# A mixture-of-experts kernel: 8 KB runs for the output matrices, and another order inside a pair of experts

## The chip, the cores and the metric

The kernel runs on one core of one Trainium2 chip. A core has five engines: TensorE (PE in the profile; PEld are its weight loads), VectorE (DVE), ScalarE (ACT), GpSimd (POOL) and SyncE (SP), which here issues the DMAs. Sixteen DMA engines move data between HBM and the on-chip buffer. The metric is the device time of one execution in microseconds, from the first to the last instruction of the core, and of several runs the median.

## The reference

Two blocks follow each other on 256 tokens of 1024 floats: two hybrid layers (convolution, attention), then an attention layer with a mixture of experts. The change lies in the experts alone. Each token goes to 4 of 32 experts; each expert has an input matrix of 1024 x 2048 and an output matrix of 1024 x 1024, all float32 (12 MB an expert, 403 MB in all):

```python
def expert_block(args):
    xb, e = args
    hcat = xb @ w_in[e] + b_in[e]
    x_glu = jnp.minimum(hcat[:, :D_FF], SWIGLU_LIMIT)
    x_lin = jnp.clip(hcat[:, D_FF:], -SWIGLU_LIMIT, SWIGLU_LIMIT)
    act = x_glu * jax.nn.sigmoid(SWIGLU_ALPHA * x_glu) * (x_lin + 1)
    return act @ w_out[e] + b_out[e]

ys = lax.map(expert_block, (xs, block_exp)).reshape(n_rows, dm)
y = jax.ops.segment_sum(ys * row_gate[:, None].astype(ys.dtype), row_tok, num_segments=n + 1)[:n]
```

The rows of `xs` are the tokens sorted by expert; `row_gate` is the weight of the token at that expert. A residual and a final norm follow.

## The kernel before

All 256 tokens stay on the chip and the weights of all 32 experts are streamed through it once. `moe` (from L1252) goes through 16 pairs of experts; each expert has 64 places for tokens, and a pair's 128 places fill the 128 rows of a tile. A branch after pair 10 (`overflow`, L1433) handles an expert with more than 64 tokens; in the profiled execution its body isn't run.

A weight tile is 1 MB, 128 partitions x 2048 floats. A pair has 24 of them, in the order in which PE needs them: 8 input tiles of the first expert, 8 of the second, then 8 output tiles, the two experts taking turns. `mload` (L1221) issues one DMA for a tile on SP into the next of 19 buffers that go round (`mv`, `mhch`, `mhcl`, `mXM`, `mtb`, `mhh`, `mhl`, `mM`, `mkbT`, `mG`, two `mY`, a second `mv`, three `mr`, three `mw`); it has to wait until PE has read what that buffer held. An input tile is 128 rows of the matrix, so each partition gets one run of 8 KB. An output tile is 256 rows of 1024 floats: partition p gets row p and row 128 + p, two runs of 4 KB (L1242). The last pair (p == 15) has its output matrices cut by columns as well, in runs of 2 KB.

One pair (`pair`, L1362) does this:

- the input matmuls (L1377), 8 tiles of each expert. `hp` holds two PSUM tiles, the gate half (i = 0) and the linear half (i = 1); each has the left 512 columns in its partitions 0 to 63 and the right 512 in 64 to 127. The biases are put there before by matmuls with a one-hot column (`in_bias`, L1330);
- the swiglu of an expert on DVE and ACT: `g` (L1383), tanh (L1384), three steps of `ln` (L1385 to L1387);
- transposes of `ln` on PE (L1391) and a copy by ACT to `aT` (L1392); after the first expert also those of the gates, `gsT` (L1398);
- the dispatch of the next pair (`dispatch`, L1336; matmuls L1354): a one-hot matrix `sx`, made by DVE (L1346), picks the next pair's tokens into `xT`, copied by ACT (L1357);
- the output matmuls (L1427; L1417 in the last pair): `aT` of the first expert writes partitions 0 to 63 of `yp`, that of the second 64 to 127;
- the combine: DVE scales `yp` to `ys` (L1407), and matmuls with `gsT` add it to the four accumulators `y` of the tokens (L1291).

PE's matmuls are fp32, so that one matmul shows up as two instructions in the profile. Matmuls that write different halves of the partitions stand side by side in the array and run at the same time.

The order in the code is not the order on the engines. A scheduler reorders all instructions by the code's order, priorities and simulated times, and fixes a sequence for each engine; an engine then takes its instructions in that sequence and waits at one that isn't ready. Four PSUM buffers, used in turn, serve `hp`, the transposes, the dispatch and `yp`.

Of the kernel before, what the change touches and what calls it, by code (L numbers as in the profile page):

```python
# [8 lines left out]
F32 = mybir.dt.float32  # L9
# [20 lines left out]
class Net:  # L30
# [1191 lines left out]
    def mload(self):  # L1222
# [11 lines left out]
        else:  # L1234
# [7 lines left out]
            src = w.rearrange("(k p) n -> p k n", p=128)  # L1242
            dst = b.rearrange("p (k n) -> p k n", k=4 if p == 15 else 2)
# [117 lines left out]

    def pair(self, disp, nxt, oh, hp, tile_of, gt2, acc, steps=(), last=False):  # L1362
        nc, T = self.nc, self.tmp
        xT, gs = disp
        hs = [slice(0, 64), slice(64, 128)]
        aT = []
        for e in range(2):
            hg, hn = hp
            for k in range(8):
                if k == 4 and e == 0:  # L1370
                    for _ in steps:
                        pass
                w = tile_of()
                for i in range(2):
                    for h in range(2):
                        o = i * 1024 + h * 512
                        nc.tensor.matmul(hp[i][hs[h]], xT[:, k, hs[e]], w[:, o:o + 512], start=False, stop=(k == 7))  # L1377
            if e == 0:
                hp = self.in_bias(oh[1])
            g = T.tile([128, 512], F32, name="g", tag="g", bufs=TB)  # L1380
            th = self.modr[:, 1]
            ln = T.tile([128, 512], F32, name="ln", tag="ln", bufs=TB)
            nc.vector.tensor_scalar(g, hg, 7.0, None, op0=ALU.min)  # L1383
            nc.scalar.activation(th, g, AF.Tanh, scale=0.851)  # L1384
            nc.vector.tensor_scalar(ln, hn, 7.0, -7.0, op0=ALU.min, op1=ALU.max)  # L1385
            nc.vector.scalar_tensor_tensor(ln, ln, 1.0, g, op0=ALU.add, op1=ALU.mult)  # L1386
            nc.vector.scalar_tensor_tensor(ln, th, 1.0, ln, op0=ALU.add, op1=ALU.mult)  # L1387
            a = T.tile([128, 4, 128], F32, name="aT", tag="aT", bufs=2)
            p = self.mm_ps([128, 4, 128])
            for c in range(4):  # L1390
                nc.tensor.transpose(p[:, c], ln[:, c * 128:(c + 1) * 128], self.ident)  # L1391
            nc.scalar.activation(a, p, AF.Copy, scale=0.5)  # L1392
            aT.append(a)
            if e == 0:
                gsT = T.tile([128, 2, 128], F32, name="gsT", tag="gsT", bufs=1)
# [200 lines left out]
```

## Time and profile before

| what | value |
|---|---|
| median of 3 runs (lowest to highest) | 2032.47 us (2032.28 to 2037.36) |
| profiled execution: span | 2031.7 us |
| PE busy | 1901.2 us (94%) |
| DVE, ACT, POOL busy | 920.7, 613.0, 410.8 us |
| HBM read | 565.8 MB |
| expert stage | about 1070 us to the end |

The profiled execution's own time is its span; the median of the runs lies 0.8 us above. Matmul ends are modelled, so that a PE that is shown as busy may still wait a little inside. A wait that the profile gives to `issue` has no releaser that it shows. Shares of DMA can be a little over 1, since packets of one engine overlap.

### The profile page before, as it was taken

The page shows a single profiled execution, that of the slowest core. Times are in us where ns is not written, and L with a number is a line of the kernel's source. Part 1 is how long each engine was busy: PE and PEld are TensorE (multiplying, and loading weights), DVE is VectorE, ACT ScalarE, POOL GpSimd, SP SyncE. Part 2 cuts the span into 40 slices and gives each one's busy share as a digit, 9 for nine tenths or more (in the row PEclk, how much of TensorE's full clock was granted, in tenths as well). Part 3 has the DMA queues.
Part 4 walks back from the last instruction along what each step waited for, and adds up shares of the span by engine and source line. Part 5 has one row for each costly group of instructions (what it writes and reads, how often), then busy time and mean ns, then how long its engine had stood idle before and what let it go on. Part 6 is the DMA issues. An engine that isn't in the chain of part 4 may idle for free. (4 is left out here: it accounts for less than half of the span.)

```text
span 2031.7 us, 25905 instructions
## 1 busy us (share of the span) xinstructions
PE 1901.2 (94%) x10323; PEld 1187.0 (58%) x10323; DVE 920.7 (45%) x1728; ACT 613.0 (30%) x1099; POOL 410.8 (20%) x334
## 2 busy tenths in 40 slices
PE   6989999989899999799969999999999998999997
PEld 6878988978679889676644333333333333333332
DVE  6798787678876665778751111111111101110102
ACT  4646445546465454455541000000000000100001
POOL 3134346653245245312120000000000000000000
PEclk8989999999899999899989999999999998999999
DMA  6545544546456435455459999999999999999994
GB/s 222 185 137 167 179 153 157 198 169 210 160 169 221 140 128 198 148 171 151 160 202 371 394 405 415 418 419 416 416 416 416 417 418 416 416 416 416 417 416 150
DMA packets 153812, 568.59 MB, mean 280 GB/s; under 512 B 10603, under 2 KB 16747, under 8 KB 120918
## 3 DMA queue, kind: packets, MB, share of 16 engines
q1 hardware_dynamic: 145024, 540.69, 69.4%
q0 software_dynamic: 6912, 25.17, 3.7%
q8 instruction: 83, 1.36, 0.3%
q10 hardware_dynamic: 1750, 1.03, 0.2%
q14 instruction: 43, 0.35, 0.1%
HBM read 565.79 MB, written 1.05 MB: 279 GB/s over the span
## 5 line engine op out<-in xcount | busy, mean ns | idle before, releaser
L158 DVE TENSOR_TENSOR wl<-raw,wh 128x1024 fp32r<-128x1024 f32 (+3 forms) x255 | 343.4, 1350 | 126.7 <-ACT wh L156 122.5
L156 ACT ACTIVATE wh<-raw 128x1024 fp32r<-128x1024 f32 (+3 forms) x255 | 262.8, 1034 | 236.9 <-PE mm L181 221.3
L1384 ACT ACTIVATE modr<-g 128x512 f32<-128x512 f32 x32 | 20.1, 629 | 675.2 <-DVE g L1383 675.2
L1383 DVE TENSOR_SCALAR g<-mm 128x512 f32<-128x512 f32 x32 | 22.1, 692 | 441.3 <-PE mm L1377 441.3
L182 PE MATMUL mm<-hh,wl 128*128 128x256 f32 x768 | 220.7, 289 | 0.9 <-DVE wl L158 0.9
L181 PE MATMUL mm<-hl,wh 128*128 128x256 f32 x768 | 220.2, 287 | 0.0
L180 PE MATMUL mm<-hh,wh 128*128 128x256 f32 x768 | 219.8, 287 | 0.0
L1304 POOL PARTITION_BROADCAST mtb<-bi x1 | 1.3, 1306 | 919.8 <-PE mm L1377 919.8
L181 PE MATMUL mm<-wl,hh 128*128 128x512 f32 (+2 forms) x424 | 173.5, 410 | 12.9 <-DVE wl L158 12.8
L182 PE MATMUL mm<-wh,hl 128*128 128x512 f32 (+2 forms) x424 | 171.5, 405 | 2.1 <-DVE hl L216 1.2
L180 PE MATMUL mm<-wh,hh 128*128 128x512 f32 (+2 forms) x424 | 164.4, 410 | 5.8 <-ACT hh L248 2.7
L822 POOL TENSOR_TENSOR araw<-araw,tb 128x1024 f32<-128x1024 f32 x48 | 100.1, 2085 | 297.7 <-DVE part L818 126.2
L182 PEld LDWEIGHTS mm<-hh,wl 128*128 128x128 f32 x768 | 144.3, 189 | 7.5 <-issue 4.4
L180 PEld LDWEIGHTS mm<-hh,wh 128*128 128x128 f32 x768 | 144.9, 189 | 4.7 <-issue 4.2
L181 PEld LDWEIGHTS mm<-hl,wh 128*128 128x128 f32 x768 | 144.7, 188 | 3.4 <-issue 2.0
L1407 DVE TENSOR_TENSOR ys<-kaT,mm 128x512 f32<-128x512 f32 x16 | 11.0, 688 | 249.5 <-PE mm L1427 239.3
L181 PEld LDWEIGHTS mm<-wl,hh 128*128 128x128 f32 x424 | 85.9, 203 | 33.3 <-DVE wl L158 15.7
L180 PEld LDWEIGHTS mm<-wh,hh 128*128 128x128 f32 x424 | 85.3, 203 | 25.8 <-ACT hh L248 4.4
L182 PEld LDWEIGHTS mm<-wh,hl 128*128 128x128 f32 x424 | 85.7, 202 | 19.3 <-DVE hl L249 2.1
L1354 PE MATMUL mm<-modr,vb 128*128 128x128 f32 x512 | 73.9, 313 | 14.1 <-DVE lg L1189 13.5
L824 POOL TENSOR_TENSOR araw<-araw 128x512 f32<-128x512 f32 x48 | 85.6, 1783 | 3.8
L1354 PEld LDWEIGHTS mm<-modr,vb 128*128 128x128 f32 x512 | 72.2, 228 | 16.2 <-DVE lg L1189 13.7
(444 smaller groups left out, 3578.0 us busy)
## 6 DMA issues: line engine op xcount, KB each, us to landing
raw<-in_w_in_dram SPq DMA_DIRECT2D x84, 1024.0 KB, 5.1
mr<-in_w_in_dram SPq DMA_DIRECT2D x41, 1024.0 KB, 18.3
mw<-in_w_in_dram SPq DMA_DIRECT2D x39, 1024.0 KB, 20.0
mv<-in_w_in_dram SPq DMA_DIRECT2D x27, 1024.0 KB, 19.9
mY<-in_w_in_dram SPq DMA_DIRECT2D x26, 1024.0 KB, 19.8
araw<-in_w_ada_dram POOLq DMA_DIRECT2D x48, 512.0 KB, 4.3
mw<-in_w_out_dram SPq DMA_DIRECT2D x21, 1024.0 KB, 19.9
mr<-in_w_out_dram SPq DMA_DIRECT2D x19, 1024.0 KB, 19.3
```

What stands on the lines that cost most here:

```text
L156: nc.scalar.activation(wh, src, AF.Copy)
L158: eng.tensor_tensor(wl, src, wh.bitcast(F32), op=ALU.subtract)
L180: nc.tensor.matmul(out, sh, mh, start=first, stop=False, skip_group_check=skip)
L181: nc.tensor.matmul(out, sh, ml, start=False, stop=False, skip_group_check=skip)
L182: nc.tensor.matmul(out, sl, mh, start=False, stop=last, skip_group_check=skip)
L822: nc.gpsimd.tensor_tensor(raw, raw, cT[:, 0, kh * 4:kh * 4 + 4, None].to_broadcast([128, 4, 256]), op=ALU.mult)
L824: nc.gpsimd.tensor_tensor(raw[:, 0:2], raw[:, 0:2], raw[:, 2:4], op=ALU.add)
L1304: nc.gpsimd.partition_broadcast(gfin, self.bi[96:97], channels=128)
L1354: nc.tensor.matmul(p[:, j], self.h2[:, t, k * 128:(k + 1) * 128], sx[:, t].rearrange("p e c -> p (e c)"), start=(t == 0 and j == 0), stop= ...
L1383: nc.vector.tensor_scalar(g, hg, 7.0, None, op0=ALU.min)
L1384: nc.scalar.activation(th, g, AF.Tanh, scale=0.851)
L1407: nc.vector.tensor_tensor(ys[:, h], gt2[h], yp[h], op=ALU.mult)
```

## The change

Three things change, all in the expert stage.

First, an output tile (but for the last pair) is read as `(p k) n`: partition p gets rows 2p and 2p + 1 of the 256, one run of 8 KB. The contraction index of the output matmuls is then spread over the partitions in another way, so that the transposes have to deliver it likewise: `act_T` transposes every second column of `ln`.

Second, `pair` is written in another order. The loop over the two experts is gone; its parts are `in_tile`, `swiglu` and `act_T`. The first expert's transposes and those of the gates are written inside the second expert's tiles, behind its tile k = 2. The next pair's dispatch comes behind the second expert's last tile, and the second expert's transposes behind the dispatch.

Third, `tc.issue_after(mm.ins)` fixes that what is written inside it comes behind that matmul in PE's sequence (without waiting for it to end).

The same reading of the output matrix is put into `overflow`.

```diff
@@ -1239,8 +1239,10 @@
                 w = w[q * 512:(q + 1) * 512, h * 512:(h + 1) * 512]
             else:
                 w = w[f * 256:(f + 1) * 256]
-            src = w.rearrange("(k p) n -> p k n", p=128)
-            dst = b.rearrange("p (k n) -> p k n", k=4 if p == 15 else 2)
+            if p == 15:
+                src, dst = w.rearrange("(k p) n -> p k n", p=128), b.rearrange("p (k n) -> p k n", k=4)
+            else:
+                src, dst = w.rearrange("(p k) n -> p (k n)", p=128), b
         if n == 383:
             for k in range(2):
                 self.nc.sync.dma_start(dst[:, 2 * k:2 * k + 2], src[:, 2 * k:2 * k + 2])
@@ -1359,47 +1361,66 @@
                 yield xT, gs
         nc.vector.tensor_tensor(gs, sx, gt[:, :, :, None].to_broadcast(full), op=ALU.mult)
 
+    def in_tile(self, hp, xT, w, k, cols):
+        for i in range(2):
+            for h in range(2):
+                o = i * 1024 + h * 512
+                mm = self.nc.tensor.matmul(hp[i][h * 64:h * 64 + 64], xT[:, k, cols], w[:, o:o + 512], start=False,
+                                           stop=(k == 7))
+        return mm
+
+    def swiglu(self, hp):
+        nc, T = self.nc, self.tmp
+        hg, hn = hp
+        g = T.tile([128, 512], F32, name="g", tag="g", bufs=TB)
+        th = self.modr[:, 1]
+        ln = T.tile([128, 512], F32, name="ln", tag="ln", bufs=TB)
+        nc.vector.tensor_scalar(g, hg, 7.0, None, op0=ALU.min)
+        nc.scalar.activation(th, g, AF.Tanh, scale=0.851)
+        nc.vector.tensor_scalar(ln, hn, 7.0, -7.0, op0=ALU.min, op1=ALU.max)
+        nc.vector.scalar_tensor_tensor(ln, ln, 1.0, g, op0=ALU.add, op1=ALU.mult)
+        nc.vector.scalar_tensor_tensor(ln, th, 1.0, ln, op0=ALU.add, op1=ALU.mult)
+        return ln
+
+    def act_T(self, ln, last):
+        nc = self.nc
+        a = self.tmp.tile([128, 4, 128], F32, name="aT", tag="aT", bufs=2)
+        p = self.mm_ps([128, 4, 128])
+        for c in range(4):
+            o = c // 2 * 256 + c % 2
+            src = ln[:, c * 128:(c + 1) * 128] if last else ln[:, o:o + 255:2]
+            nc.tensor.transpose(p[:, c], src, self.ident)
+        nc.scalar.activation(a, p, AF.Copy, scale=0.5)
+        return a
+
     def pair(self, disp, nxt, oh, hp, tile_of, gt2, acc, steps=(), last=False):
         nc, T = self.nc, self.tmp
         xT, gs = disp
         hs = [slice(0, 64), slice(64, 128)]
+        for k in range(8):
+            if k == 4:
+                for _ in steps:
+                    pass
+            self.in_tile(hp, xT, tile_of(), k, hs[0])
+        ln0 = self.swiglu(hp)
+        hp = self.in_bias(oh[1])
         aT = []
-        for e in range(2):
-            hg, hn = hp
-            for k in range(8):
-                if k == 4 and e == 0:
-                    for _ in steps:
-                        pass
-                w = tile_of()
-                for i in range(2):
-                    for h in range(2):
-                        o = i * 1024 + h * 512
-                        nc.tensor.matmul(hp[i][hs[h]], xT[:, k, hs[e]], w[:, o:o + 512], start=False, stop=(k == 7))
-            if e == 0:
-                hp = self.in_bias(oh[1])
-            g = T.tile([128, 512], F32, name="g", tag="g", bufs=TB)
-            th = self.modr[:, 1]
-            ln = T.tile([128, 512], F32, name="ln", tag="ln", bufs=TB)
-            nc.vector.tensor_scalar(g, hg, 7.0, None, op0=ALU.min)
-            nc.scalar.activation(th, g, AF.Tanh, scale=0.851)
-            nc.vector.tensor_scalar(ln, hn, 7.0, -7.0, op0=ALU.min, op1=ALU.max)
-            nc.vector.scalar_tensor_tensor(ln, ln, 1.0, g, op0=ALU.add, op1=ALU.mult)
-            nc.vector.scalar_tensor_tensor(ln, th, 1.0, ln, op0=ALU.add, op1=ALU.mult)
-            a = T.tile([128, 4, 128], F32, name="aT", tag="aT", bufs=2)
-            p = self.mm_ps([128, 4, 128])
-            for c in range(4):
-                nc.tensor.transpose(p[:, c], ln[:, c * 128:(c + 1) * 128], self.ident)
-            nc.scalar.activation(a, p, AF.Copy, scale=0.5)
-            aT.append(a)
-            if e == 0:
-                gsT = T.tile([128, 2, 128], F32, name="gsT", tag="gsT", bufs=1)
-                p = self.mm_ps([128, 2, 128])
-                for t in range(2):
-                    nc.tensor.transpose(p[:, t], gs[:, t].rearrange("p e c -> p (e c)"), self.ident)
-                nc.scalar.activation(gsT, p, AF.Copy)
+        for k in range(8):
+            mm = self.in_tile(hp, xT, tile_of(), k, hs[1])
+            if k == 2:
+                with self.tc.issue_after(mm.ins):
+                    aT.append(self.act_T(ln0, last))
+                    gsT = T.tile([128, 2, 128], F32, name="gsT", tag="gsT", bufs=1)
+                    p = self.mm_ps([128, 2, 128])
+                    for t in range(2):
+                        nc.tensor.transpose(p[:, t], gs[:, t].rearrange("p e c -> p (e c)"), self.ident)
+                    nc.scalar.activation(gsT, p, AF.Copy)
+        ln1 = self.swiglu(hp)
         hp = None
         if nxt is not None:
-            nxt = self.dispatch(*nxt)
+            with self.tc.issue_after(mm.ins):
+                nxt = self.dispatch(*nxt)
+        aT.append(self.act_T(ln1, last))
         yp = [self.mm_ps([128, 512]) for _ in range(2)]
         ys = T.tile([128, 2, 512], F32, name="ys", tag="ys", bufs=YB)
 
@@ -1479,8 +1500,8 @@
                         else:
                             f = (i - 16) // 2
                             src = d["w_out_2"][bass.ds(e, 1), f * 256:(f + 1) * 256]
-                            src = src.rearrange("o p n -> (o p) n").rearrange("(k p) n -> p k n", p=128)
-                            nc.gpsimd.dma_start(b.rearrange("p (k n) -> p k n", k=2), src)
+                            src = src.rearrange("o p n -> (o p) n").rearrange("(p k) n -> p (k n)", p=128)
+                            nc.gpsimd.dma_start(b, src)
                         return b
 
                     self.pair(disp, None, [one, one], hp, tile_of, gt2, combine)
```

The sequences of PE, at three places. The numbers of lines are each kernel's own: L1377, L1391, L1398, L1354, L1427 and L1330 of before are L1368, L1392, L1416, L1356, L1448 and L1332 after. `x4` is four matmuls in a row.

PE in pair 12 before, from the second expert's first tile (in `mv_10485`) to its transposes:

```order
L1377 MATMUL mm<-mv_10485,xT 64x512 x4
L1391 MATMUL mm<-ident,ln 128x128 x4
L1398 MATMUL mm<-ident,modr 128x128 x2
L1377 MATMUL mm<-mr,xT 64x512 x12
L1377 MATMUL mm<-mw_10699,xT 64x512 x4
L1377 MATMUL mm<-mw_10700,xT 64x512 x4
L1377 MATMUL mm<-mw_10701,xT 64x512 x4
L1377 MATMUL mm<-mY_10885,xT 64x512 x4
L1391 MATMUL mm<-ident,ln 128x128 x4
```

And after, from the same tile on:

```order
L1368 MATMUL mm<-mv_10485,xT 64x512 x4
L1368 MATMUL mm<-mr,xT 64x512 x8
L1392 MATMUL mm<-ident,ln 128x128 x4
L1416 MATMUL mm<-ident,modr 128x128 x2
L1368 MATMUL mm<-mr,xT 64x512 x4
L1368 MATMUL mm<-mw_10699,xT 64x512 x4
L1368 MATMUL mm<-mw_10700,xT 64x512 x4
L1368 MATMUL mm<-mw_10701,xT 64x512 x4
L1368 MATMUL mm<-mY_10885,xT 64x512 x4
L1356 MATMUL mm<-modr,vb 128x128 x16
L1392 MATMUL mm<-ident,ln 128x128 x4
```

The first expert's transposes and the gates' stand behind three of the second expert's tiles and no longer behind one; the dispatch (L1354, now L1356) stands ahead of the second expert's transposes.

PE in pair 12 before, from the dispatch into the output matmuls (L1427):

```order
L1354 MATMUL mm<-modr,vb 128x128 x16
L1427 MATMUL mm<-mv_8426,aT 64x512
L1427 MATMUL mm<-mhch,aT 64x512
L1427 MATMUL mm<-mv_8426,aT 64x512
L1427 MATMUL mm<-mhch,aT 64x512
L1427 MATMUL mm<-mv_8426,aT 64x512
L1427 MATMUL mm<-mhch,aT 64x512
L1427 MATMUL mm<-mv_8426,aT 64x512
L1427 MATMUL mm<-mhch,aT 64x512
L1427 MATMUL mm<-mhcl,aT 64x512 x2
L1330 MATMUL mm<-bi,ident 64x512 x4
L1427 MATMUL mm<-mXM,aT 64x512 x2
```

And after:

```order
L1356 MATMUL mm<-modr,vb 128x128 x16
L1392 MATMUL mm<-ident,ln 128x128 x4
L1448 MATMUL mm<-mv_8426,aT 64x512 x2
L1332 MATMUL mm<-bi,ident 64x512 x2
L1448 MATMUL mm<-mhch,aT 64x512 x2
L1448 MATMUL mm<-mv_8426,aT 64x512
L1448 MATMUL mm<-mhch,aT 64x512
L1448 MATMUL mm<-mv_8426,aT 64x512
L1448 MATMUL mm<-mhch,aT 64x512
L1332 MATMUL mm<-bi,ident 64x512 x2
L1448 MATMUL mm<-mhcl,aT 64x512 x2
L1448 MATMUL mm<-mXM,aT 64x512 x2
```

The first group of output matmuls, in which the two experts took turns, now begins with two of the first expert, two bias matmuls and two of the second expert.

PE in pair 0 before, from the second expert's last tile into the output matmuls:

```order
L1377 MATMUL mm<-mw_10699,xT 64x512 x4
L1391 MATMUL mm<-ident,ln 128x128 x4
L1354 MATMUL mm<-modr,vb 128x128 x16
L1427 MATMUL mm<-mw_10700,aT 64x512
L1427 MATMUL mm<-mw_10701,aT 64x512
L1427 MATMUL mm<-mw_10700,aT 64x512
L1427 MATMUL mm<-mw_10701,aT 64x512
L1427 MATMUL mm<-mw_10700,aT 64x512
L1427 MATMUL mm<-mw_10701,aT 64x512
```

And after:

```order
L1368 MATMUL mm<-mw_10699,xT 64x512 x4
L1356 MATMUL mm<-modr,vb 128x128 x16
L1392 MATMUL mm<-ident,ln 128x128 x4
L1448 MATMUL mm<-mw_10700,aT 64x512 x2
L1332 MATMUL mm<-bi,ident 64x512 x2
L1368 MATMUL mm<-mhh,xT 64x512 x2
L1368 MATMUL mm<-mhl,xT 64x512 x2
L1368 MATMUL mm<-mM,xT 64x512 x2
L1368 MATMUL mm<-mkbT,xT 64x512 x2
L1368 MATMUL mm<-mG,xT 64x512
L1448 MATMUL mm<-mw_10701,aT 64x512 x2
L1448 MATMUL mm<-mw_10700,aT 64x512
```

Two bias matmuls and the first matmuls on five of the next pair's tiles (`mhh` to `mG`) have moved between the first output matmuls. In pair 1 there are three such tiles, in later pairs none. SP issues the same tiles in the same order as before, and DVE's sequence is unchanged; on ACT the two copies to `xT` stand ahead of the second expert's copy to `aT` instead of behind it.

## Rows read from the trace of the kernel before

**Rows 1.** the page, bandwidth in 40 equal slices of the span

```profile
GB/s 222 185 137 167 179 153 157 198 169 210 160 169 221 140 128 198 148 171 151 160 202 371 394 405 415 418 419 416 416 416 416 417 418 416 416 416 416 417 416 150
```

**Rows 2.** stretches: us, busy us (x instructions) by engine, PEclk, DMA share, GB/s

```profile
1500.00:1600.00 100.00, 93.98 (x438) 37.85 (x437) 13.90 (x24) 7.22 (x13) 0.00 (x0) 0.98 1.02 417
```

**Rows 3.** stretches, the end of the weight stream

```profile
2000.00:2002.00 2.00, 0.05 (x1) 0.06 (x1) 1.75 (x3) 0.23 (x1) 0.00 (x0) 1.00 0.11 40
2002.00:2004.00 2.00, 2.00 (x8) 1.07 (x10) 0.00 (x0) 0.60 (x1) 0.00 (x0) 0.82 0.00 0
```

**Rows 4.** instructions on tile mv, last pair: ns min/median/max, first and last

```profile
L1417 PEld LDWEIGHTS mm<-mv,aT x4: 133/136/137, 2010.7 to 2014.8; 128*64 128x64 f32 x4
...
L1248 SPq DMA_DIRECT2D mv<-in_w_out_dram x1: 2447/2447/2447, 1979.9 to 1979.9; - x1
...
DMA to landing us min/median/max: 14.3/14.3/14.3
```

**Rows 5.** timeline of the end: start us, us, engine, line, operation, tiles

```profile
2020.79 1.02 PE L1417 MATMUL mm<-mXM,aT 128*64 128x512 f32 x2
...
2021.85 0.69 DVE L1407 TENSOR_TENSOR ys<-va,mm 128x512 f32<-128x512 f32 x1 [5.54 <-PE mm L1417]
```

**Rows 6.** waits of PE from 1200 to 2000: us, times, longest

```profile
PE mm L1391 <- DVE ln L1387: 37.0, 23, 2.3
PE mm L1330 <- PEq L1447: 4.6, 1, 4.6
```

**Rows 7.** timeline of DVE, first expert of pairs 3 and 10

```profile
1259.47 0.69 DVE L1383 TENSOR_SCALAR g<-mm 128x512 f32<-128x512 f32 x1 [17.11 <-PE mm L1377]
...
1677.24 0.69 DVE L1383 TENSOR_SCALAR g<-mm 128x512 f32<-128x512 f32 x1 [18.18 <-PE mm L1377]
```

**Rows 8.** stretches with output tiles alone, then with input tiles alone

```profile
1254.00:1269.00 15.00, 15.00 (x74) 4.96 (x72) 3.19 (x5) 1.50 (x3) 0.00 (x0) 1.00 1.03 408
...
1555.00:1570.00 15.00, 14.31 (x70) 5.00 (x68) 3.19 (x5) 1.50 (x3) 0.00 (x0) 1.00 1.03 409
...
1285.00:1300.00 15.00, 15.00 (x76) 4.73 (x74) 1.67 (x3) 0.60 (x1) 0.00 (x0) 1.00 1.02 422
...
1585.00:1600.00 15.00, 15.00 (x67) 5.23 (x64) 1.38 (x2) 0.00 (x0) 0.00 (x0) 1.00 1.01 420
```

**Rows 9.** timeline of PE in pair 13, idle time before in brackets

```profile
1867.03 0.63 PE L1391 MATMUL mm<-ident,ln 128*128 128x128 f32 x4 [0.69 <-DVE ln L1387]
...
1869.57 1.89 PE L1377 MATMUL mm<-mY,xT 128*64 128x512 f32 x8
1871.29 1.89 PE L1377 MATMUL mm<-mv,xT 128*64 128x512 f32 x8
...
1882.36 0.66 PE L1391 MATMUL mm<-ident,ln 128*128 128x128 f32 x4 [2.31 <-DVE ln L1387]
```

**Rows 10.** chain of work that ended last, in pair 13: start us, us, what

```profile
1883.01 3.57 PE mm L1354 x32
1886.59 3.58 PE mm L1427 x16
1890.17 1.00 PE mm L1330 x4
1891.17 1.86 PE mm L1427 x4
...
1894.04 10.45 PE mm L1427 x44
```

**Rows 11.** stretches around the second expert's transposes in pair 14

```profile
1939.60:1941.90 2.30, 0.02 (x2) 0.00 (x0) 2.08 (x3) 0.63 (x1) 0.00 (x0) 0.98 1.03 426
1941.90:1945.20 3.30, 3.26 (x16) 3.26 (x16) 0.00 (x0) 0.60 (x1) 0.00 (x0) 0.50 1.01 420
```

**Rows 12.** stretch of pair 1

```profile
1140.00:1150.00 10.00, 10.00 (x43) 2.95 (x44) 1.93 (x3) 0.63 (x1) 0.00 (x0) 0.84 0.80 299
```

**Rows 13.** stretch in the router, ahead of the expert stage

```profile
1040.00:1050.00 10.00, 6.79 (x69) 4.22 (x67) 4.51 (x19) 3.31 (x9) 1.48 (x2) 1.00 0.84 324
```

## The prediction, made before the changed kernel ran

> **What bounds the kernel now.** I read the slices of the page first. In their last half the bandwidth is flat at 416 to 419 GB/s up to the last slice [rows 1]: the expert stage, from about 1070 us on, streams its weights without a pause. The table by stretches agrees: a DMA share of 1.02 with PE busy 94 of 100 us [rows 2]. So two things look like the bound, and the end of the trace has to decide. The DMA share is 0.11 between 2000 and 2002 us and 0.00 after [rows 3]: the last weight lands at about 2002.0. PE is then still far behind. The buffer `mv` of the last pair, issued at 1979.9, landed 14.3 us later, at 1994.2, and PE first read it at 2010.7 [rows 4], 16.5 us after it was there; PE's last expert matmuls start at 2020.8 [rows 5]. The waits of PE between 1200 and 2000 us name no DMA at all, only the vector engine's swiglu (37.0 us in 23 waits) and the branch of the overflow test (4.6) [rows 6]. The DMA engines run all the time because 19 buffers lie between them and PE, but the end is set by PE, which comes in some 20 us behind the last weight. The first expert's `g` is at 1259.47 in pair 3 and at 1677.24 in pair 10 [rows 7], so PE takes 417.8 / 7 = 59.7 us a pair.
>
> DMA needs nearly the same. While only output tiles (4 KB runs) move, the rate is 408 and 409 GB/s in the first and last of six stretches (six together: 409.0); while only input tiles (8 KB runs) move, 422 and 420 (420.7) [rows 8]. One 1.0486 MB tile is then 2.564 us in 4 KB runs and 2.493 in 8 KB runs; a pair of 16 input and 8 output tiles is 60.4 us.
>
> **The change, part by part.**
>
> Output tiles. An output tile gets the access pattern that an input tile has now, so I give it the input tile's rate: 0.071 us less a tile. 117 of the 120 changed tiles lie behind the stream's start (three are loaded before PE begins): 117 x 0.071 = 8.3 us, all on the DMA path, none on PE's. A pair costs DMA 59.8. By the single rows the bounds are 0.067 (420 against 409: 7.9 us) and 0.085 (422 against 408: 10 us); a loss is excluded, since 256 such tiles run so now. The last landing comes to 2002.0 - 8.3 = 1993.7.
>
> The first expert's transposes. They stand one tile after the first expert now and wait 0.69 us for `ln`; 1867.03 is such a wait [rows 9]. In the new order three tiles stand before them; a tile is 1.72 us of PE (1869.57 to 1871.29 [rows 9]), and `ln` is ready 2.3 us after the expert's last matmul, so 5.1 us cover it. Minus 0.69 a pair, with 2.8 us of cover to spare.
>
> The next dispatch ahead of the second expert's transposes. These wait 2.31 us now (1882.36 [rows 9]) with PE idle. The dispatch (32 passes, 3.57 us [rows 10]) moves into this hole; it needs nothing of the swiglu, its one-hot is made by DVE a pair earlier, and DVE's order is unchanged. Minus 2.31 a pair. What is late next: `aT` of the second expert, copied by ACT behind its transposes, was hidden by the dispatch, and ACT now has the two `xT` copies ahead of it. In the new order PE fills this with two matmuls of the first expert and a bias, 1.86 + 1.00 us, so it is covered. That has a price: two matmuls of one expert fill half the columns of the array, where those of the two experts run side by side. The same splitting stands in the kernel before: 3.58 us for a side-by-side group, then 1.00, 1.86, 1.00 and 10.45 [rows 10], 17.9 together. The new order gives 1.86 + 1.00 + 3.43 (the group's other six) + 1.00 + 10.45 + 0.86 (a matmul for each expert that the 10.45 lack) = 18.6: plus 0.7. The transposes now read every second column of `ln`; no row shows that. I take the stride at nothing, as the nearest row has transposes without it at 0.66 for four [rows 9]; if it doubled them it would be 1.1 us a pair with the loads, and it can't gain.
>
> PE's sum: 0.69 + 2.31 - 0.7 = 2.3 us a pair. It holds for pairs 3 to 9 and 11 to 14, 11 x 2.3 = 25.3. Pair 10 (no dispatch) and pair 15 keep their 2.31. Pairs 0 to 2 have their first transposes inside already and pay for the splitting; I give them 3 us together, from pair 0. PE without any wait for data would end at 2031.7 - 28.3 = 2003.4. With the stride's 12 us it is 2015. Below: behind such a hole PE drops to 1.2 GHz, idle from 1939.6 to 1941.9 and then 3.3 us at a granted clock of 0.50 [rows 11], 1.7 us lost in about every second pair; if filling the hole ends that, 5 x 1.7 = 8 us more, 1995.
>
> Hoisted input. In pair 0 the first matmuls of five of the next pair's tiles move ahead of most output matmuls. The output tiles' buffers come free some 2.5 us later, and SP's next issue with them: DMA dries up for about 2 us near 1113. Against that, the hole at 1140 (share 0.80, 2.0 us [rows 12]) closes, since those five tiles are then free earlier. I take the sum as nothing, between -2 and +4.
>
> The sum. After the last half tile lands, three matmuls remain (two of 0.86 behind each other) with some latency, 1.9 us, then the combine and the final norm as now: from `ys` at 2021.85 [rows 5] to 2031.7, 9.85 us. With DMA: 1993.7 + 11.8 = 2005.5. With PE alone: 2003.4. The later one sets the end, and the two meet only 2 us apart; for pairs in which PE has to wait unevenly I add 0.8. Span 2006.3. The median of the runs is 0.8 us above the profiled span (2032.47 against 2031.7): 2007 us, 1.25% less. Part of what PE gains comes back as a new wait for weights.
>
> **Rules weighed.** Rows 8 show 4 KB runs 2.8% slower than 8 KB runs. The Trainium skill (DMA: Bandwidth & Descriptors, Specifications) names 512 B as the transfer from which line rate is had; by it the 0.071 would be nought. The measurement decides against it here. The same page (Why small descriptors are slow) counts three extra beats a packet; an estimate by that page, two packets of 128 beats against one of 256, is 1.2%, 0.03 us a tile, 3.5 us in all.
>
> **Rivals.**
>
> PE stays the bound (20%). For: the stride or the splitting cost more than I gave them, or ACT's copies come late. With the stride's 1.1 us a pair PE ends at 2015; with 2 us a pair lost, 2003.4 + 22 = 2025. Time 2011 to 2026. Against: each cover above has its row.
>
> The runs' length doesn't matter to DMA (7%): the last landing stays at 2002.0, the end is 2013.8, the median 2015. For: rows 8 could come from something else in which output tiles differ. Against: after the change nothing in their pattern differs from an input tile's. The skill's 512 B would give this one.
>
> DMA gains more (9%): 10 us and the closed hole, 2002.
>
> PE's clock falls while it waits for weights (4%, slower). PE never waits for a DMA now; once it has caught up it waits up to 0.77 us a tile (2.49 less 1.72). If the granted clock fell in these waits as it does behind the 2.3 us hole, each such stretch would cost 1.7 us. PE's pair is 57.4, DMA's 59.8: 2.4 us of slack. To end where it does now, a pair must lose that and 2.2 more (26 us over 12 pairs), about three stretches. With four: 6.8 - 2.4 = 4.4 x 12 pairs, 2007 + 53 = 2060. For: rows 11. Against: between 1040 and 1050 us PE was busy 6.79 of 10 us, in short pieces, at a clock of 1.00 [rows 13]; and at 1.2 GHz a tile is 3.4 us of PE, so it would no longer wait. The Trainium skill (TensorE: Matmul & The Clock Gate, Loop structure matters more than you think) has this as its bad loop: "long DMA wait between every matmul → PE goes cold". [...]
>
> **How the numbers follow.** DMA sets the end, 2003 to 2011 (the forecast): 58%. PE stays the bound 20%, no DMA gain 7%, more DMA gain 9%, clock 4%; 2% for no effect, both gains lost (within 0.3%, about what a measurement of this kernel can tell from no change: 2026 to 2039). The range of 1999 to 2020 takes in the bounds of DMA and of the holes and more than half of the PE rival; 3% lie below, some 13% above. Faster by over 0.3%: all but the clock, the no-effect case and the slow end of the PE rival, 92%; same 4%, slower 4%.
>
> **What would show it.** In the profile after: output tiles at 418 to 422 GB/s; waits for `ln` only in pairs 10 and 15; the dispatch straight behind the second expert's last tile; waits of PE for DMA, some 2 us a pair, from the middle pairs on; the last landing at 1992 to 1996 and the last `ys` about 2 us behind it. I am wrong if the last weights wait 10 us or more for PE as now, if output tiles stay near 409 GB/s, or if the granted clock falls in the middle of input tiles.

## The result, and the profile after

The changed kernel takes 2005.82 us (median of 4 runs, 2004.15 to 2007.06) against 2032.38 us before (4 runs): a ratio of 0.9864, with a 95% interval of 0.9845 to 0.9882. Forecast was 2007, with 1999 to 2020 as the range. The profiled execution has a span of 2002.5 us.

The bandwidth slices of the page after answer to [rows 1]:

```profile
GB/s 225 185 140 159 190 158 148 211 168 198 171 169 212 137 160 159 192 148 147 168 231 291 407 380 421 421 420 420 421 421 421 420 421 420 420 421 421 421 421 291
```

A stretch from the middle of the expert stage, as in [rows 2] (us, busy us by engine, granted clock, DMA share, GB/s):

```profile
1500.00:1600.00 100.00, 100.00 (x451) 37.99 (x452) 13.83 (x23) 6.12 (x11) 0.00 (x0) 1.00 1.01 421
```

The flat rate went from 417 to 421 GB/s, and PE, which was busy 93.98 of these 100 us, is busy in all of them. That the runs are longer stands in the DMA line of each page, first of before and then of after:

```profile
DMA packets 153812, 568.59 MB, mean 280 GB/s; under 512 B 10603, under 2 KB 16747, under 8 KB 120918
```

```profile
DMA packets 138452, 568.59 MB, mean 284 GB/s; under 512 B 10603, under 2 KB 16747, under 8 KB 90198
```

30,720 packets under 8 KB are gone, which is 120 tiles of 256, for half as many of 8 KB. The waits of PE from 1200 us to the end answer to [rows 6] (total us, times, longest):

```profile
PE mm L1392 <- DVE ln L1382: 4.6, 2, 2.3
PE mm L1332 <- PEq L1468: 4.6, 1, 4.6
PE mm L1368 <- DMA mr<-in_w_in_dram: 1.7, 3, 0.6
PE mm L1438 <- DMA mY<-in_w_out_dram: 1.5, 1, 1.5
...
PE mm L1368 <- DMA mkbT<-in_w_in_dram: 0.8, 2, 0.6
PE mm L1448 <- DMA mw<-in_w_out_dram: 0.6, 1, 0.6
```

In the same stretch of before the waits for the swiglu were 39.3 us (37.0 of them ahead of 2000, as in [rows 6]); 4.6 are left, the holes of pairs 10 and 15. Waits for weights are there for the first time, 5.7 us together. The chain of work in pair 12 shows why the holes are gone:

```profile
1786.24 0.68 PE mm L1392 x4
1786.92 0.22 PE mm L1416 x2
1787.14 8.73 PE mm L1368 x40
1795.87 3.77 PE mm L1356 x32
1799.64 0.47 PE mm L1392 x4
1800.12 1.86 PE mm L1448 x4
1801.98 1.00 PE mm L1332 x4
1802.98 3.58 PE mm L1448 x12
1806.56 1.00 PE mm L1332 x4
1807.56 10.50 PE mm L1448 x48
```

The dispatch (L1356) stands right behind the second expert's last tile, its transposes (second L1392) follow with no gap, and so do the output matmuls (L1448). The first expert's `g` in pairs 4 and 10 gives the period, as [rows 7] did:

```profile
1313.37 0.69 DVE L1378 TENSOR_SCALAR g<-mm 128x512 f32<-128x512 f32 x1 [18.18 <-PE mm L1368]
```

```profile
1653.48 0.69 DVE L1378 TENSOR_SCALAR g<-mm 128x512 f32<-128x512 f32 x1 [18.18 <-PE mm L1368]
```

340.1 us for six pairs is 56.7 us a pair, where it was 59.7. At the end, three stretches and the last `ys`, answering to [rows 3, 5]:

```profile
1984.00:1988.00 4.00, 4.00 (x16) 1.29 (x16) 1.38 (x2) 1.38 (x4) 0.00 (x0) 1.00 0.58 219
1988.00:1990.00 2.00, 2.00 (x12) 0.70 (x10) 0.00 (x0) 0.00 (x0) 0.00 (x0) 1.00 0.21 81
1990.00:1992.00 2.00, 2.00 (x11) 0.58 (x8) 0.00 (x0) 0.00 (x0) 0.00 (x0) 1.00 0.00 0
```

```profile
1992.65 0.69 DVE L1428 TENSOR_TENSOR ys<-va,mm 128x512 f32<-128x512 f32 x1 [5.54 <-PE mm L1438]
```

The DMA engines move weights until just before 1990, and the last `ys` starts some 3 us later; before, 20 us lay between the two. The last weight now sets the end.

**A part of the profiled difference isn't the change's.** One of the router's last steps on DVE is the second `lg`. Up to it PE's order is the same in all kernels here. It starts at 1061.5 us in the trace of before and at 1055.8 in that of after (first and last start us):

```profile
L1189 DVE SCALAR_TENSOR_TENSOR lg<-mm,rm,cst x2: 239/245/251, 1042.9 to 1061.5; 128x32 f32<-128x32 f32 x2
```

```profile
L1189 DVE SCALAR_TENSOR_TENSOR lg<-mm,rm,cst x2: 239/245/251, 1036.6 to 1055.8; 128x32 f32<-128x32 f32 x2
```

So 5.7 of the 29.2 us between the spans arose ahead of the expert stage. Over the ten other traces below it lay anywhere between 1054.9 and 1066.2. From here on I call the rest of a span, from that instruction to the end, the stage: 970.2 us before, 946.7 after, 23.5 less; the forecast had 25.4 of the span. A second trace of the changed kernel gave 946.5.

### The profile page after: what moved, and what is told of

Same layout as the page of the kernel before. It is cut to its first block, busy times and chain, and to the rows that moved or that the text cites. A ratio compares the mean times of both kernels' runs of the same rounds, so it can differ in the third digit from the quotient of the medians.

```text
span 2002.5 us, 25915 instructions
## 1 busy us (share of the span) xinstructions
PE 1907.1 (95%) x10323; PEld 1182.0 (59%) x10323; DVE 916.5 (46%) x1728; ACT 609.9 (30%) x1099; POOL 411.6 (21%) x334
## 5 line engine op out<-in xcount | busy, mean ns | idle before, releaser
L158 DVE TENSOR_TENSOR wl<-raw,wh 128x1024 fp32r<-128x1024 f32 (+3 forms) x255 | 339.2, 1334 | 126.8 <-ACT wh L156 123.0
L822 POOL TENSOR_TENSOR araw<-araw,tb 128x1024 f32<-128x1024 f32 x48 | 104.7, 2180 | 299.0 <-DVE part L818 123.2
L180 PEld LDWEIGHTS mm<-wh,hh 128*128 128x128 f32 x424 | 84.0, 200 | 26.4 <-ACT hh L248 5.2
L1356 PE MATMUL mm<-modr,vb 128*128 128x128 f32 x512 | 65.8, 289 | 14.7 <-DVE lg L1189 14.1
L1368 PE MATMUL mm<-mr,xT 128*64 128x512 f32 x328 | 78.1, 604 | 1.7 <-DMA mr<-in_w_in_dram 1.7
## 6 DMA issues: line engine op xcount, KB each, us to landing
mr<-in_w_out_dram SPq DMA_DIRECT2D x19, 1024.0 KB, 19.9
```

What stands on the lines that cost most here:

```text
L158: eng.tensor_tensor(wl, src, wh.bitcast(F32), op=ALU.subtract)
L180: nc.tensor.matmul(out, sh, mh, start=first, stop=False, skip_group_check=skip)
L822: nc.gpsimd.tensor_tensor(raw, raw, cT[:, 0, kh * 4:kh * 4 + 4, None].to_broadcast([128, 4, 256]), op=ALU.mult)
L1356: nc.tensor.matmul(p[:, j], self.h2[:, t, k * 128:(k + 1) * 128], sx[:, t].rearrange("p e c -> p (e c)"), start=(t == 0 and j == 0), stop= ...
L1368: mm = self.nc.tensor.matmul(hp[i][h * 64:h * 64 + 64], xT[:, k, cols], w[:, o:o + 512], start=False, stop=(k == 7))
```

## The experiments

| kernel | median us | ratio to before on the same chip, 95% interval | router ends | span | stage |
|---|---|---|---|---|---|
| before | 2032.38 | | 1061.5 | 2031.7 | 970.2 |
| changed | 2005.82 | 0.9864 (0.9845 to 0.9882) | 1055.8 | 2002.5 | 946.7 |
| changed, again | 2008.18 | 0.9874 (0.9847 to 0.9902) | 1060.8 | 2007.3 | 946.5 |
| 8 KB runs alone | 2037.45 | 1.0032 (1.0019 to 1.0046) | 1059.1 | 2035.1 | 976.0 |
| order alone | 2012.30 | 0.9913 (0.9893 to 0.9934) | 1055.9 | 2010.1 | 954.2 |
| dispatch behind | 2025.67 | 0.9961 (0.9941 to 0.9981) | 1066.2 | 2033.9 | 967.7 |
| no hoisting | 2006.37 | 0.9870 (0.9850 to 0.9889) | 1061.9 | 2005.1 | 943.2 |
| sums later too | 2000.97 | 0.9839 (0.9811 to 0.9868) | 1057.9 | 1999.7 | 941.8 |
| first transposes early | 2005.38 | 0.9861 (0.9832 to 0.9890) | 1060.4 | 2004.8 | 944.4 |
| input in 4 KB runs | 2024.84 | 0.9965 (0.9944 to 0.9986) | 1059.9 | 2023.6 | 963.7 |
| 8 KB runs, old transposes | 2032.10 | 0.9992 (0.9974 to 1.0010) | 1059.2 | 2032.1 | 972.9 |
| strided transposes alone | 2035.41 | 1.0001 (0.9987 to 1.0015) | 1054.9 | 2031.1 | 976.2 |

**The two halves of the change, each by itself.** First the kernel before with the 8 KB runs:

```diff
-            src = w.rearrange("(k p) n -> p k n", p=128)
-            dst = b.rearrange("p (k n) -> p k n", k=4 if p == 15 else 2)
+            if p == 15:
+                src, dst = w.rearrange("(k p) n -> p k n", p=128), b.rearrange("p (k n) -> p k n", k=4)
+            else:
+                src, dst = w.rearrange("(p k) n -> p (k n)", p=128), b
...
-                nc.tensor.transpose(p[:, c], ln[:, c * 128:(c + 1) * 128], self.ident)
+                o = c // 2 * 256 + c % 2
+                src = ln[:, c * 128:(c + 1) * 128] if last else ln[:, o:o + 255:2]
+                nc.tensor.transpose(p[:, c], src, self.ident)
```

> The kernel before with one thing of the change: output tiles as 8 KB runs, and transposes of every second column to match. Theory (PE sets the end, the runs lie on the DMA path alone): PE keeps its 59.5 to 60.1 us a pair and its 2.3 and 0.7 us holes; the output tiles move at 420 GB/s instead of 409, so the last weight lands some 9 us earlier and waits some 9 us longer for PE; time 2032, between 2029 and 2034, that is no change. Rival A (the end follows the DMA engines even before): 2023. Rival B (the strided transposes cost PE about 1 us a pair): 2043 or more.

It came out 3.8 us slower than before on its chip (2033.65). PE's waits from 1200 us on have the old pattern, with no DMA in it:

```profile
PE mm L1395 <- DVE ln L1389: 39.3, 24, 2.3
PE mm L1332 <- PEq L1451: 4.7, 1, 4.7
```

Faster weights alone bring nothing while PE sets the end; rival A falls. The last landing was expected some 9 us earlier, and that was a miss: counted from the router's end, the last weight packet ends only 1.0 us earlier than before. The stream runs at 420 to 421 GB/s from 1200 to 1700 us, but at 396 between 1700 and 1800. SP waited 618 us for PE to read buffers between 1200 and 2000 us, where it was 232 before: the weights can run ahead of PE only as far as there are buffers. The small loss is taken up again below. Then the changed kernel with the old runs and transposes, which leaves the new order:

```diff
-            if p == 15:
-                src, dst = w.rearrange("(k p) n -> p k n", p=128), b.rearrange("p (k n) -> p k n", k=4)
-            else:
-                src, dst = w.rearrange("(p k) n -> p (k n)", p=128), b
+            src = w.rearrange("(k p) n -> p k n", p=128)
+            dst = b.rearrange("p (k n) -> p k n", k=4 if p == 15 else 2)
...
-            o = c // 2 * 256 + c % 2
-            src = ln[:, c * 128:(c + 1) * 128] if last else ln[:, o:o + 255:2]
-            nc.tensor.transpose(p[:, c], src, self.ident)
+            nc.tensor.transpose(p[:, c], ln[:, c * 128:(c + 1) * 128], self.ident)
```

> The changed kernel with the old 4 KB runs of the output tiles and the old transposes of neighbouring columns; order of a pair as changed. Theory (once PE's holes are gone the DMA engines set the end): output tiles at 409 GB/s again, 117 tiles x 0.08 us = 9 us later than the changed kernel: 2015, between 2012 and 2017, with PE waiting for DMA some 15 us in all instead of 6. Rival (the order is all of the gain, PE sets the end in both): 2006, as the changed kernel.

2012.3: between the theory's 2015 and the rival's 2006, in the theory's range. Its stretch and some of its waits for weights:

```profile
1500.00:1600.00 100.00, 100.00 (x451) 37.47 (x451) 13.34 (x22) 6.12 (x11) 0.00 (x0) 1.00 1.02 418
```

```profile
PE mm L1366 <- DMA mr<-in_w_in_dram: 1.7, 3, 0.6
PE mm L1434 <- DMA mY<-in_w_out_dram: 1.5, 1, 1.5
...
PE mm L1366 <- DMA mhcl<-in_w_in_dram: 1.1, 2, 0.6
PE mm L1366 <- DMA mXM<-in_w_in_dram: 1.1, 2, 0.6
```

All waits for weights add up to 11.1 us, against 5.7 in the changed kernel. The longer runs are thus worth 954.2 - 946.7 = 7.5 us of the stage once the order is new, and nothing with the old order. The gains of the halves don't add: the order moves the bound from PE to the DMA engines, and the runs move the new bound.

**Which step of the order.** The dispatch back behind the second expert's transposes:

```diff
+        aT.append(self.act_T(ln1, last))
         if nxt is not None:
-            with self.tc.issue_after(mm.ins):
+            with self.tc.issue_after(self.tr.ins):
                 nxt = self.dispatch(*nxt)
-        aT.append(self.act_T(ln1, last))
```

Here `self.tr` is the last transpose of `act_T`.

> The changed kernel with one step of the order taken back: the next pair's dispatch stands behind the second expert's transposes again, so that these wait for the swiglu with PE idle. Theory (the 2.31 us hole is what PE gained most): the hole is back in every pair, PE takes 59.0 us a pair instead of 56.7 (plus the stretches at half clock behind it), never waits for DMA, and sets the end: the kernel before less the first expert's 0.69 us in some 11 pairs, 2024, between 2019 and 2028. Rival (the 8 KB runs are the gain, DMA sets the end anyway): 2006 to 2009.

2025.67, as the theory has it. From 1200 us on there are 14 holes, where the changed kernel has 2, and nothing waits for DMA:

```profile
PE mm L1392 <- DVE ln L1382: 32.4, 14, 2.3
PE mm L1332 <- PEq L1468: 4.8, 1, 4.8
```

Of the stage's 23.5 us, 967.7 - 946.7 = 21.0 hang on this one step; that trace is of one of the slowest of its runs (2035.57), and by the medians, of two chips, it is 19.9. The other step, the first expert's transposes behind three tiles, was undone like this:

```diff
-            mm = self.in_tile(hp, xT, tile_of(), k, hs[1])
-            if k == 2:
+            w = tile_of()
+            with self.tc.issue_after((self.tr if k == 1 else mm).ins) if k else nullcontext():
+                mm = self.in_tile(hp, xT, w, k, hs[1])
+            if k == 0:
```

> The changed kernel with the first expert's transposes behind one tile of the second expert instead of three, so that they wait about 0.7 us for the swiglu again, in every pair. Theory (PE waits for DMA 5.7 us in all at the end of the changed kernel, so it has that much slack): 15 x 0.7 = 10 us more on PE, 5.7 of it hidden, about 4 us more on the end: 2010, between 2007 and 2012. Rival A (DMA alone sets the end): 2006, no change. Rival B (PE alone sets it): 2016.

2005.38 beside 2008.18 for the changed kernel on the same chip, and a stage 2.1 us shorter: this step brings nothing to the end. The theory was wrong in its sum, and rival A came true. The small holes are there, 12 more:

```profile
PE mm L1392 <- DVE ln L1382: 12.9, 14, 2.3
```

A pair takes 57.4 us instead of 56.7, by `g`, so that pairs 4 to 9 and 11 to 13 lost 6.6 us together. Against the second trace of the changed kernel 8.7 came back elsewhere: 0.4 ahead of the first `g`, 2.5 in pairs 0 to 2 (179.6 to 177.1), 2.6 in pair 10 (69.8 to 67.2), 1.0 in pair 14, and 2.2 from the last `g` to the end. PE's waits for weights, which fell from 4.6 to 1.5 us, are a part of the last three. I had counted these waits as PE's only slack.

**What keeps the DMA engines from running through.** In the changed kernel the first halves of five and three of the next pair's tiles stand among the output matmuls of pairs 0 and 1. They were kept behind the last output matmul:

```diff
-            self.in_tile(hp, xT, tile_of(), k, hs[0])
+            w, out = tile_of(), getattr(self, "out_mm", None)
+            with self.tc.issue_after(out.ins) if out is not None else nullcontext():
+                self.in_tile(hp, xT, w, k, hs[0])
...
+        self.out_mm = None if nxt is None else mm
```

> The changed kernel, but the next pair's input tiles are kept behind this pair's last output matmul, which takes out the first halves of five and three tiles that stood among the output matmuls of pairs 0 and 1. Theory (they hold back the output tiles' buffers, SP waits for these, and the DMA engines run dry for 2.5 us in pair 0 and about 5 us in pair 1): these gaps shrink by about 2.5 us each, the last landing comes 2 to 5 us earlier, time 2002, between 2000.5 and 2004. Rival A (the gaps only move to the next place where PE is behind): 2005 to 2006.5, no change. Rival B (PE used this work to cover its wait for the second expert's copy): PE waits there, 2007 to 2010.

By the times this is no change (2006.37, another chip than the first runs), as rival A has it and not the theory; in the stage, by this one trace, it is 3.5 us less. The next kernel also moves the matmuls that add the residual and the biases to the accumulators out of pair 0:

```diff
             if q == 0:
                 self.counts()
+            if q == 5:
                 base()
```

> The changed kernel with the next pair's input tiles kept behind this pair's last output matmul, and with the residual and bias matmuls of the accumulators (some 7.5 us of PE, in pair 0 now) moved to pair 5. Theory (DMA sets the end, and its engines run dry in pairs 0 and 1 only because PE is late there in giving buffers back): what is left of these gaps goes, the weights land some 4 to 6 us earlier than in the changed kernel counted from the router's end; time 2001, between 1999 and 2003.5. Rival (PE has no slack left, so that it sets the end when the weights come earlier): 2005 to 2007.

2000.97, as the theory has it: five runs from 1999.31 to 2001.58, each below all six of the changed kernel on that chip (2002.55 to 2012.36). It is the fastest kernel here. Three stretches of 100 us, each from 25 us after its router's end, of the changed kernel, of the one without hoisting, and of this one:

```profile
1081.00:1181.00 100.00, 100.00 (x447) 38.98 (x444) 12.05 (x22) 7.37 (x14) 0.00 (x0) 0.98 0.95 393
```

```profile
1087.00:1187.00 100.00, 100.00 (x452) 39.40 (x450) 13.41 (x24) 7.38 (x14) 0.00 (x0) 1.00 1.00 410
```

```profile
1083.00:1183.00 100.00, 100.00 (x458) 39.08 (x454) 13.42 (x24) 7.00 (x13) 0.00 (x0) 1.00 1.01 420
```

393, 410 and 420 GB/s: 6.4 us of the DMA engines' time had been lost there ((420 - 393) / 420 x 100), and 4.9 of it came back in the stage.

**Does PE's clock fall while it waits for weights?** The waits of the changed kernel are few, so the input tiles were put in 4 KB runs, which slows the weights:

```diff
-            src, dst = d["w_in_2"][e, k * 128:(k + 1) * 128], b
+            w = d["w_in_2"][e, k // 2 * 256:k // 2 * 256 + 256, k % 2 * 1024:k % 2 * 1024 + 1024]
+            src, dst = w.rearrange("(k p) n -> p k n", p=128), b.rearrange("p (k n) -> p k n", k=2)
```

> The changed kernel with the input tiles read as two 4 KB runs per partition, from other places of the input matrices (256 rows by 1024 columns a tile), so that what it computes is not the reference. Theory (DMA sets the end; a 4 KB run tile costs 0.07 to 0.08 us more; waits of PE for weights leave its clock alone): 235 tiles x 0.071 = 17 us later, 2023, between 2020 and 2026, the stream at 409 GB/s throughout, PE waiting some 15 to 25 us for DMA in all, in pieces of under 1 us, at a granted clock of 1.00. Rival (the clock falls to 0.50 in stretches in which PE waits for weights): several drops a pair outside pairs 10 and 15, and PE late by 50 us or more, 2060. Rival B (the length of the run is nothing to DMA): 2006.

2024.84, and a stage 17.0 us longer, which was the forecast (the output tiles kept their 8 KB runs, so 413 GB/s and not 409 is the mean of the stream). The edit also takes a tile's rows from other places of the matrix, which no run here separates from the length of the runs. PE waited 18.6 us for weights in all. Two pairs in which it waits at most tiles:

```profile
1540.00:1660.00 120.00, 114.24 (x512) 41.81 (x510) 15.26 (x24) 7.63 (x14) 0.00 (x0) 1.00 1.02 413
```

```profile
PE mm L1369 <- DMA mr<-in_w_in_dram: 2.8, 5, 0.6
PE mm L1369 <- DMA mw<-in_w_in_dram: 2.5, 4, 0.6
```

5.8 us of 120 are idle, in pieces of 0.6 us or less, and the granted clock is 1.00.

**What made the 8 KB runs alone slower.** Their two parts again, in the kernel before; PE's order is the same in all of these. First the new runs with the old transposes (the first half of that diff), then the strided transposes with the old runs (its second half):

> The kernel before with output tiles as 8 KB runs and the old transposes of neighbouring columns, so that the output matrix's rows and the activations don't match and the result is not the reference's. It takes the strided transposes out of the run with 8 KB runs alone, which came out 3.8 us slower than before; PE's order is the same in all of them. Theory (that loss was the stride, whose weight loads took 209 ns instead of 140): 2033, between 2030 and 2035, no change against before. Rival (it was the earlier weights themselves, or the clock behind the holes): 2036 to 2039.

> The kernel before with the strided transposes alone, output tiles in 4 KB runs as before (result not the reference's, since rows and activations don't match). Theory (the stride costs PE 0.2 to 0.3 us a pair where PE sets the end): 2037, between 2035 and 2039. Rival (the stride costs nothing, the transposes being bound by something else): 2032 to 2034.

2032.10 and 2035.41. Both agree with the theory, but the second has an interval of 0.9987 to 1.0015 about no change, so the times alone don't settle it. The stages lean its way: 976.2 with the stride alone and 976.0 with stride and runs, with the same period in nearly every pair, against 972.9 with the runs alone and 970.2 before. Weight loads and matmuls of the transposes (ns min/median/max), of before and with the stride:

```profile
L1391 PEld LDWEIGHTS mm<-ident,ln x128: 138/140/230, 1089.2 to 2002.2; 128*128 128x128 f32 x128
L1391 PE MATMUL mm<-ident,ln x128: 272/273/475, 1089.2 to 2002.3; 128*128 128x128 f32 x128
```

```profile
L1393 PEld LDWEIGHTS mm<-ident,ln x128: 139/209/231, 1083.5 to 2003.4; 128*128 128x128 f32 x128
L1393 PE MATMUL mm<-ident,ln x128: 272/283/488, 1083.5 to 2003.5; 128*128 128x128 f32 x128
```

A load takes 209 ns instead of 140. In pairs at full clock that is about 0.2 us a pair (59.8 against 59.6 by `g`), 3 us in all. The rest of the 6 us fits the clock, which falls to half 13 times in each of these two stages and 11 times before; such a fall costs 1.6 us, as the last section shows. How much of the 3.8 us is the stride's and how much the spread of the runs stays open.

## Point by point

**The bound before** was read rightly. With PE's holes the 8 KB runs alone brought nothing, though their weights moved at 421 GB/s; the flat DMA share was not the limit.

**The output tiles** were given 8.3 us (bounds 7.9 and 10). The runs showed 7.5 in the stage. By the 512 B of the Trainium skill (DMA: Bandwidth & Descriptors, Specifications) it would have been nothing; the runs don't agree, since 4 KB runs were slower than 8 KB ones in the input tiles too, by 17.0 us. The estimate from that page's three cycles a packet (Why small descriptors are slow), 3.5 us, is half of what was measured.

**The second expert's hole** is the step that carried the change: 2.31 us a pair as forecast. **The first expert's** 0.69 us went as forecast too, but its return cost nothing at the end.

**The price of the split output matmuls** was taken from one pair and put on all. In the changed kernel these matmuls take 17.9 us with their biases, as in pair 12 above. Before, they took as much only in pairs 4, 7, 9, 11 and 13, the last of which [rows 10] shows; there the price was nothing. The term that failed is the "0.86 that the 10.45 lack": the 44 instructions of that row already end with two matmuls of one expert by themselves (1.88 us from 1902.60), and the 48 of the new order (10.50 us) don't. In pairs 5, 6, 8, 12 and 14 a pair at full clock was 1.1 us shorter (58.5 against 59.6), and that much is lost. In pairs 0 to 3 the matmuls stood side by side throughout, 13.9 us and 1.0 for the biases, so that the price is 3.0. The output matmuls of pair 3, before and after (busy us of these alone):

```profile
1285.00:1299.00 14.00, 13.92 (x64) 4.51 (x64) 1.00 1.01 420
1276.40:1294.40 18.00, 16.09 (x64) 5.65 (x64) 1.00 1.01 421
```

Pairs 4 to 9 and 11 to 13 got 26.4 us shorter together, 2.9 each. Three of these nine had a stretch at half clock before and none has one now, which is 0.5 a pair at 1.6 us each; the other 2.4 are close to the 2.3 forecast. That filling the holes might end such stretches stands in the prediction as the lower case, and not in its sum.

**The stride** was taken at nothing with 1.1 us a pair as the other bound. It is 0.1 us a pair in the changed kernel (56.7 against 56.6 in the order alone), where DMA sets the end, so that it should cost nothing there; no run shows that by itself.

**Pairs 0 to 3** were to bring some 5 us and brought nothing: from the first `g` to that of pair 4 it took 237.9 us before and 237.5 after. Pairs 1 and 2 got longer (56.6 and 57.6 us for 55.8 and 55.8). Without hoisting they took 56.4 and 57.6, so that it is the split matmuls, at 3.0 us, that ate the gain there. **The hoisting** was taken as nothing, between -2 and +4; by one trace without it, it cost 3.5 us of the stage, near its upper bound, and the times don't show it. **Pair 10** became slower, 70.2 us against 67.7, which I had not foreseen: PE had caught up with the weights there and waited 1.3 us for them, and its output matmuls took 18.5 us instead of 15.7, 0.6 of that one of these waits.

**The two ends** were to lie 2 us apart, and that is what made the forecast hold: a miss on PE's side costs little where DMA sets the end. There was luck in it too. PE's misses nearly cancel (more than forecast in the middle pairs, 5 us less in pairs 0 to 3, a longer pair 10), and the median came within 1.2 us although the stage lost 23.5 us and not 25.4; on another chip it was 2008.18. PE waited only 5.7 us for weights over the whole stage, not 2 us a pair from the middle on: it was late by what pairs 0 to 3 and pair 10 had not gained. So DMA sets the end, as forecast, but by little. The last weight landed about 1989.7; with the router's end of before that is 1995.4, against 1993.7 forecast: 6.6 us earlier than before instead of 8.3. From there to the end it takes 12.8 us, for 11.8 forecast.

**The rival of the clock** is refuted for waits of this size: with 18.6 us of waits for weights the clock stays at 1.00. The Trainium skill's "long DMA wait between every matmul → PE goes cold" (TensorE: Matmul & The Clock Gate, Loop structure matters more than you think) is about far longer waits in its example than these of 0.6 us a tile; no run here has such a wait for weights. [rows 13] was weaker evidence than it seemed: of its 3.2 idle us, 1.7 begin a wait of 13.5 us for the router's `lg`. PE's clock did fall in that one, to 0.55 on average between 1050 and 1060 us, and behind some of the 2.3 us holes.

## What to carry to other kernels

When two resources need nearly the same time, measure each half of a change by itself: the half that works on the resource that waits shows nothing, and can still be worth nearly its full size once the other is fixed (7.5 of 8.3 us here). Fill a wait with independent work from the next step, and then look at what the scheduler moved into the gaps elsewhere, since work that comes early can hold back the buffers on which the next transfers wait. To compare small effects, count from the last instruction that the kernels share, because what lies ahead of it spreads by more than the effect.

## What the runs showed that was not expected

The traces' router ended between 1054.9 and 1066.2 us though PE's order up to there doesn't differ, while the stage of the changed kernel came out at 946.7 and 946.5. No other kernel was traced twice.

One of the 2.3 us holes of before, in pair 12, and the stretch after it:

```profile
1820.00:1822.25 2.25, 0.00 (x0) 0.00 (x0) 2.08 (x3) 0.57 (x1) 0.00 (x0) 1.00 1.01 422
1822.25:1825.65 3.40, 3.37 (x16) 3.37 (x17) 0.00 (x0) 0.60 (x1) 0.00 (x0) 0.52 1.01 419
```

After 2.25 us of idling PE gets half the clock, 1.2 GHz, for 3.4 us, but not after every such hole: after 8 of 16 before, and after 1 of the 2 that are left in the changed kernel. The cost shows where the same pair, in the same order of PE, has such a stretch in one trace and not in another. Pair 13 before, and in the kernel with 8 KB runs and old transposes, with the stretch that only the latter has (the first expert's `g` of pairs 13 and 14 in each, then the stretch):

```profile
1863.81 0.69 DVE L1383 TENSOR_SCALAR g<-mm 128x512 f32<-128x512 f32 x1 [18.18 <-PE mm L1377]
1923.39 0.69 DVE L1383 TENSOR_SCALAR g<-mm 128x512 f32<-128x512 f32 x1 [18.18 <-PE mm L1377]
```

```profile
1864.27 0.69 DVE L1385 TENSOR_SCALAR g<-mm 128x512 f32<-128x512 f32 x1 [18.18 <-PE mm L1379]
1925.48 0.69 DVE L1385 TENSOR_SCALAR g<-mm 128x512 f32<-128x512 f32 x1 [18.18 <-PE mm L1379]
1884.10:1887.50 3.40, 3.40 (x19) 3.40 (x18) 0.00 (x0) 0.61 (x2) 0.00 (x0) 0.51 1.02 419
```

61.2 us with the stretch and 59.6 without: it costs 1.6 us, close to the 1.7 of the prediction. In pair 14 it is the other way round, 58.4 without and 60.0 with.

The runs of one kernel spread widely: 23 runs of before on one chip went from 2025.5 to 2043.4 us, twelve with the dispatch behind from 2019.0 to 2037.1. The fastest kernel stayed within 2.3 us in five runs, but the one with 4 KB input runs, which has no more holes, went over 13.8 us in ten, so that the holes alone don't explain the spread. The stretches at half clock agree with a part of it: in the three sets of before (17 and twice 23 runs) the slower runs have the lower granted clock (correlation -0.82, -0.65 and -0.58), by 1.5 to 2.4 us for each 0.001. By my estimate one stretch lowers the mean over a run by 0.0008 (half of 3.4 us in 2030), so that its 1.6 us would make 1.9 us for each 0.001. Whether these stretches make the spread was not tried.
